# Gates and branch projections with tokens on partitions, and a transposed merge, in a hybrid decoder block

## The chip, the cores and the metric

One core of a Trainium2 chip runs the whole block. The metric is device time in microseconds, the median of several executions; a profile is one further execution recorded by the hardware. TensorE (PE in the profile) multiplies matrices into PSUM, VectorE (DVE) and ScalarE (ACT) do the elementwise work, GpSimd (POOL) nearly nothing here, and SyncE (SP) issues the weight loads. Each engine works through its own instructions in order.

## The reference

One layer over 256 tokens of width 2048, in float32: a mixer sub-layer, then a squared-ReLU MLP. The change lies in the mixer's gates and merge.

```python
h = rms_norm(x, mix_norm_pre) * (1.0 + sc1) + sh1          # sc1, sh1, g1, ... = silu(c) @ w_ada + b_ada
a_q, a_f, a_i, a_g, b_q, b_k, b_v, c_a, c_g = split_cols(h @ w_in, IN_SPLITS)
ya = hgrn2_mixer(...)                # (256, 1024)
yb = dilated_attention_mixer(...)    # (256, 256)
yc = conv_module(...)                # (256, 768)
gates = sigmoid(h @ w_gate + b_gate).reshape(256, 3, 2048)
merged = (gates[:, 0] * (ya @ w_a_out) + gates[:, 1] * (yb @ w_b_out)
          + gates[:, 2] * (yc @ w_c_out))
x = x + g1 * rms_norm(merged @ w_o, mix_norm_post)
h = rms_norm(x, mlp_norm_pre) * (1.0 + sc2) + sh2
x = x + g2 * rms_norm(square(relu(h @ w_up)) @ w_down, mlp_norm_post)
```

## The kernel before

**Jobs.** All weight matrices are cut into chunks of 512 KB (128 partitions x 1024 float32: two k tiles of 128 rows by 512 columns), and each chunk is one job. `run` (L176) goes through one long list of jobs. For each it issues the loads up to five jobs ahead on SyncE's queue into a ring of six raw tiles (`load`, L110), then the splits up to four jobs ahead (`SA`), then the job's own matmuls, then a little side work (`work`, L146). A split (`split`, L117) makes two parts of a weight: ScalarE casts the raw tile to a rounded high part (L126), VectorE subtracts it to give the low part (L127). Activations are kept in the same two parts, and each product takes three matmuls: high x high, high x low, low x high.

**Two forms of a job.** `mm_a` (L240) holds 128 weight columns in the array and moves 256 tokens past them; the result has weight columns on partitions. For a chunk that is 2 k tiles x 4 column tiles x 3 products = 24 matmuls of 256 columns (L252 to L254). `mm_b` (L256) holds 128 tokens and moves 512 weight columns; the result has tokens on partitions: 2 k tiles x 2 token tiles x 3 = 12 matmuls of 512 columns (L264 to L266).

**The order of the jobs.** Input projection with the first adaLN products; then 96 gate jobs (`gj`: four strips n of 512 output columns, in each three branches b of eight chunks; the eight chunks of one (b, n) are a unit), 32 projection jobs (`pj`: in each strip four chunks of ya, one of yb, three of yc), 32 jobs of the output projection (`oj`), 128 of the MLP's up, 128 of its down projection. The list is gates of strips 0 to 2, projection of strip 0, gates of strip 3, projection of strips 1 to 3, output projection. From the 33rd gate job on, 96 adaLN jobs are woven in (L1084): each loads 512 KB too, and VectorE alone multiplies and sums it (L297). When a group of them is done, `g_finish` (L835) writes 2 KB as 4-byte elements to a DRAM scratch (L841) and reads it back as a row on all 128 partitions (L843), both on ScalarE's queue, so that ScalarE stands until the write has landed.

**Side work.** HGRN, attention and convolution are generators in two lists, `chain` (with hand-overs between engines) and `filler` (VectorE alone). After each job `work` takes steps from them, at fixed places of the program:

```python
for _ in range(CH_STEPS):             # CH_STEPS = 2
    c = step(chain)
    if c is None: break
    budget -= c * CH_COST
while budget > 0: ...                 # filler
while budget > 0 and not filler:
    c = step(chain)
    if c is None: break
    budget -= c
```

The instructions are then put in their final order on each engine when the program is built, by a list scheduler that prefers what was written first and can let a later instruction pass one that it expects to wait.

**Gates** (`gate_job`, L814) use `mm_a`. After the eighth chunk ScalarE applies the sigmoid out of PSUM, four times 128x256, with the bias as an operand per partition (L824), which came with the constants. **Projections** (`proj_job`, L859) use `mm_a` too. After a branch's last chunk VectorE multiplies PSUM by the gate (L871) and adds to the strip's sum (L875). After the third branch ScalarE and VectorE split the sum into high and low part (L879, L880); as it has columns on partitions, `o_job` (L947) can hold it in the array directly. The first up unit (`up_job`, L1018) shows a neighbouring form: it is computed with `mm_b`, its relu goes to SBUF, and TensorE transposes it in eight 128x128 pieces (L1048).

**Pools.** `s4`: 28 tiles of 4 KB per partition. `s2`: nine tiles of 2 KB per partition. PSUM: three units of two banks (`ps_unit`) and two single banks (`bank`).

Of the kernel before, what the change touches and what calls it, by code (L numbers as in the profile page):

```python
# [26 lines left out]
# how the work is cut and interleaved  # L27
U0 = 13  # units of the input projection that run along with the first norm's modulation
# [19 lines left out]
for _n, _w in (("c", 16), ("lb", 8), ("b1", 32), ("b2", 32), ("bg1", 16), ("bg2", 16),  # L48
               ("n1", 16), ("n2", 16), ("np1", 16), ("np2", 16), ("bg", 48), ("cw", 186), ("cb", 6), ("lng", 6), ("lnb", 6),
               ("hw", 1)):  # L50
    VEC[_n] = (_o, _o + _w)
    _o += _w
# [4 lines left out]
def hybrid_block(ctx: ExitStack, tc: tile.TileContext, a, out, dbg=None):  # L57
# [57 lines left out]
    gate = []  # instructions that the splits are to come after  # L115
# [14 lines left out]
    chain = []   # (priority, order, generator): work with engine hand-overs, a few steps at a time  # L130
    filler = []  # work of the vector engine alone
# [33 lines left out]
    class Job:  # L165
        def __init__(self, src, shape, fn, ada=False, budget=1.3, keep=0, wait=False, lo_eng=None, extra=False):
            self.src, self.shape, self.fn, self.ada, self.budget = src, shape, fn, ada, budget
            self.keep = keep  # how many jobs later its split weights are let go
            self.wait = wait  # its weights are split by an earlier job's call of ahead(), or when its turn comes
            self.lo_eng = lo_eng  # L170
            self.extra = extra  # its split weights lie in the other pool
            self.raw = self.hl = None
# [54 lines left out]
    def rsqrt_col(dst, parts, scale):  # L227
        """1 / sqrt(scale * sum(parts) + eps), one column: exp(-ln / 2) and a Newton step"""
# [11 lines left out]
    def mm_a(ps, h, l, na, ah, al, first, last, tk=None):  # L240
        """ps[128 cols x 4, 256 tok] += W[kt, cols]^T . act[kt, tok]; na chunks of k in h; tk: one token tile"""
# [14 lines left out]
    def mm_b(ps, h, l, na, ah, al, first, last, tts=(0, 1)):  # L256
        """ps[tt][128 tok, cols] += act[kt, tok]^T . W[kt, cols]"""
# [17 lines left out]
    cbc = []  # silu(c) along the free axis, on every partition  # L275

    def bcast_cols(ps, cols, n):
        """ps[:, j * 128:...] = column j of cols along the free axis, on every partition"""
        for j in range(n):
            nc.tensor.matmul(ps[:, j * P:(j + 1) * P], cols[:, j:j + 1].to_broadcast([P, P]), ident, start=True, stop=True)  # L280
# [8 lines left out]
    def ada_jobs(ct0, n, finish, budget=0.0):  # L289
        """n tiles of 128 output columns on the partitions, two halves of k each along the free axis"""  # L290
# [16 lines left out]
    def ada_pe_jobs(finish):  # L307
        """the first tiles (sc 256 | sh 256) on the tensor engine: 4 groups of k in 4 column groups at once"""
# [24 lines left out]
    def mod_cols(t, kt, dst, b, nw):  # L333
        """dst[:, kt..kt+1, (0, 1)] = (1 + sc) * norm, sh"""
# [9 lines left out]
    xT = []  # L344
    hT = []  # 8 tiles [128, (hi, lo), 2 kt, 256]
# [151 lines left out]
    def lower_bounds():  # L497
        # softmax over the depth axis (one layer), cumulated, less the first layer's
# [34 lines left out]
    vt = [None] * 6  # token-layout units: [b_v 768 | a_i 1024 | a_g 1024]  # L533
# [8 lines left out]
    def hgrn_levels(half):  # L542
        F, Q, K = hg[half]
        A = s4([P, 2, 4, P])  # [s, tile, head, t]
# [97 lines left out]
    def bias_repeat():  # L642
        # row p of head h's square repeats its bias row; read back with a pitch one short, row p is shifted by p
        for h in range(12):
            b0 = bsc[h:h + 1, :]
            nc.scalar.dma_start(brep[h], bass.AP(tensor=b0.tensor, offset=b0.offset, ap=[[0, P], [1, 384]]))

    def bias_rows():
        # B_h[d] = rel_bias[bucket(d), h] where group's pattern allows d, else the mask value
# [113 lines left out]
    # ================= phase 1: first ten input units, streamed with the adaLN strips =================  # L763
# [4 lines left out]
    sj, due = [], {}  # the strips' jobs; how many of them come before the first use of h's pair j  # L768
# [7 lines left out]
    pos = []  # pace of the adaLN jobs: as even as the first uses allow  # L776
# [11 lines left out]
    # ================= phase 2: rest of the input projection (token layout) =================  # L788
# [21 lines left out]
    # ================= phase 3: gates =================  # L810
# [3 lines left out]
    def gate_job(b, n, ch):  # L814
        def fn(h, l):
            if ch == 0:
                pst["gt"] = ps_unit()
            kts = [2 * ch, 2 * ch + 1]
            mm_a(pst["gt"], h, l, 2, [h_hi(k) for k in kts], [h_lo(k) for k in kts], ch == 0, ch == 7)
            if ch == 7:  # L820
                gates[b, n] = s4([P, 4, S])
                for j in range(4):
                    c = b * 16 + n * 4 + j
                    g = nc.scalar.activation(gates[b, n][:, j, :], pst["gt"][:, j // 2, (j % 2) * S:(j % 2 + 1) * S],  # L824
                                             AF.Sigmoid, bias=V("bg")[:, c:c + 1])
                if (b, n) == (2, 3):
                    with tc.issue_after(g.ins):
# [20 lines left out]
    # ================= phase 4: branch projections, gated and merged =================  # L848
    merged = [None] * 4  # F32R [128, (hi, lo) ...]
# [8 lines left out]

    def proj_job(n, ki):  # L859
# [3 lines left out]
        def fn(h, l):  # L863
# [3 lines left out]
            mm_a(pst["pj"], h, l, 2, [t[:, 0, 0, :], t[:, 0, 1, :]], [t[:, 1, 0, :], t[:, 1, 1, :]], first, last)  # L867
            if last:
                g = gates[b, n]
                gv = g.rearrange("p a b -> p (a b)")  # L870
                nc.vector.tensor_mul(gv, pst["pj"].rearrange("p a b -> p (a b)"), gv)  # L871
# [4 lines left out]
                if b == 2:  # L876
                    mh = s4([P, 4, S], F32R)
                    ml = s4([P, 4, S], F32R)
                    nc.scalar.copy(mh, merged[n])  # L879
                    nc.vector.tensor_sub(ml, merged[n], mh.bitcast(F32))  # L880
                    mhl[n] = (mh, ml)
# [5 lines left out]
    # ================= phase 5: output projection, residual, second norm =================  # L887
    x2 = [None] * 4   # [128 tok, tt, 512]
# [18 lines left out]
    h2 = []  # (hi, lo) of four k tiles each  # L907
# [90 lines left out]
    # ================= phase 6: MLP up =================  # L998
# [4 lines left out]
    # order in which the last token tile's chain (p, g), the splits ahead (a) and the first tile's h2 (digits) are traced  # L1003
# [66 lines left out]
    def weave(main, extra):  # L1070
        """main: (jobs, share of the extra ones that goes with each of them)"""
# [19 lines left out]
    # ================= phase 7: MLP down, residual =================  # L1091
# [91 lines left out]
def _chunks(w, kt=2, cols=512):  # L1183
    """[K, N] -> [unit, chunk][128, kt * cols], contiguous"""
# [9 lines left out]
def layout(inputs):  # L1194
# [16 lines left out]
    for k in range(3):  # L1211
# [15 lines left out]
    a["wada0"] = _chunks(cat([sc1[:, :256], sh1[:, :256]], 1))  # L1227
    b = i["b_ada"][0].reshape(6, D)
# [5 lines left out]
        _cols(i["mlp_norm_post"], 16), _cols(i["b_gate"], 48), cw,  # L1234
# [16 lines left out]
```

## Time and profile before

| what | value |
|---|---|
| time, three runs | 1697.65, 1705.83, 1707.48 us |
| median | 1705.83 us |
| span of the profiled execution | 1694.7 us |
| TensorE matmuls | 1636.3 us busy (97%) |
| VectorE | 1163.1 us busy (69%) |
| ScalarE | 745.7 us busy (44%) |
| moved by DMA | 403.31 MB, mean 238 GB/s |

The span goes from the first to the last instruction of one execution. A matmul counts as busy from its start to the modelled end of its result; neighbouring matmuls overlap, so the distance of their starts, not their length, says how fast TensorE goes. Busy shares are means over stages with different limits; the windows and the chain of waits tell what limits one stage. The chain is followed back from the last instruction, at each step to what released it.

### The profile page before, as it was taken

How to read it: one execution, taken by the hardware profiler on the slowest of the kernel's cores; microseconds unless marked ns; L12 is line 12 of the kernel's file. 1: busy time of each engine (PE TensorE's matmuls, PEld its weight loads, DVE VectorE, ACT ScalarE, POOL GpSimd, SP SyncE). 2: the span in 40 equal slices, each digit the busy share in tenths (PEclk: the TensorE clock that was granted, in tenths of full speed). 3: DMA queues.
4: the chain of work that ended last, by engine and by line, in shares of the span. 5: the costliest groups of instructions: out<-in, count | busy, mean ns of one | idle time of the engine just before them, and what ended most of it. 6: DMA issues, size and time to landing. Idle time of an engine off the chain costs nothing.

```text
span 1694.7 us, 27625 instructions
## 1 busy us (share of the span) xinstructions
PE 1636.3 (97%) x11142; PEld 1511.2 (89%) x11142; DVE 1163.1 (69%) x1549; ACT 745.7 (44%) x891; POOL 11.7 (1%) x12
## 2 busy tenths in 40 slices
PE   5999999999999997999999899999999899999997
PEld 4899999878999997999988799999999788888886
DVE  5799979658899885987996755544554655444444
ACT  3644453354454443444444644434343644333333
POOL 0000000000000000000000200000000000000000
PEclk9999999999999999999999999999999999999999
DMA  7999985654344998998898377776767676565662
GB/s 283 323 333 341 326 319 181 205 177 143 101 147 140 290 305 256 360 363 314 284 360 311 125 258 226 231 214 213 247 214 233 208 232 209 190 197 191 194 194 79
DMA packets 120535, 403.31 MB, mean 238 GB/s; under 512 B 17100, under 2 KB 21080, under 8 KB 120408
## 3 DMA queue, kind: packets, MB, share of 16 engines
q1 hardware_dynamic: 107280, 388.24, 68.4%
q10 hardware_dynamic: 13128, 13.31, 2.6%
q8 instruction: 87, 1.43, 0.3%
q14 instruction: 40, 0.33, 0.1%
HBM read 397.28 MB, written 6.59 MB: 238 GB/s over the span
## 4 chain that ended last, share of the span: by engine, by line
PE 79%; DMA 9%; DVE 6%; ACT 3%; issue 2%; ACTq 0%; DVEq 0%; SPq 0%
PE g L254 14%; PE g L252 13%; PE g L253 13%; PE g L1128 5%; PE g L1126 5%; PE g L1127 5%; DMA raw<-wada 5%; PE g L266 4%; PE g L264 4%; PE g L265 4%; DVE lo L127 3%; DMA np_scratch<-adat 2%; PE m L1128 2%; PE m L1126 2%; PE m L1127 2%
## 5 line engine op out<-in xcount | busy, mean ns | idle before, releaser
L126 ACT CAST hi<-raw 128x1024 fp32r<-128x1024 f32 x538 | 561.4, 1051 | 814.9 <-PE g L253 242.6
L127 DVE TENSOR_TENSOR lo<-raw,hi 128x1024 fp32r<-128x1024 f32 x534 | 645.7, 1221 | 316.3 <-ACT hi L126 298.0
L252 PE MATMUL g<-s,hi 128*128 128x256 f32 x2560 | 728.5, 285 | 14.0 <-ACT hi L126 14.0
L254 PE MATMUL g<-s,lo 128*128 128x256 f32 x2560 | 729.2, 285 | 6.3 <-DVE lo L127 6.1
L253 PE MATMUL g<-s,hi 128*128 128x256 f32 x2560 | 727.3, 284 | 0.0
L252 PEld LDWEIGHTS g<-s,hi 128*128 128x128 f32 x2560 | 493.8, 193 | 15.1 <-ACT hi L126 15.0
L254 PEld LDWEIGHTS g<-s,lo 128*128 128x128 f32 x2560 | 493.5, 193 | 9.4 <-DVE lo L127 9.3
L253 PEld LDWEIGHTS g<-s,hi 128*128 128x128 f32 x2560 | 493.6, 193 | 0.0
L297 DVE SCALAR_TENSOR_TENSOR raw<-raw,s 128x1024 f32<-128x1024 f32 x184 | 224.0, 1219 | 130.8 <-DMA raw<-wada 130.6
L1126 PE MATMUL g<-hi,s 128*128 128x512 f32 x384 | 149.4, 389 | 0.0
L1127 PE MATMUL g<-lo,s 128*128 128x512 f32 x384 | 149.4, 389 | 0.0
L1128 PE MATMUL g<-hi,s 128*128 128x512 f32 x384 | 149.4, 389 | 0.0
L266 PE MATMUL g<-hi,s 128*128 128x512 f32 (+1 forms) x344 | 132.9, 386 | 2.9 <-DVE s L940 2.9
L264 PE MATMUL g<-hi,s 128*128 128x512 f32 (+1 forms) x344 | 132.3, 385 | 0.0
L265 PE MATMUL g<-lo,s 128*128 128x512 f32 (+1 forms) x344 | 131.6, 382 | 0.3 <-DVE lo L127 0.3
L1128 PEld LDWEIGHTS g<-hi,s 128*128 128x128 f32 x384 | 72.1, 188 | 15.0
L1127 PEld LDWEIGHTS g<-lo,s 128*128 128x128 f32 x384 | 72.0, 188 | 15.0
L1126 PEld LDWEIGHTS g<-hi,s 128*128 128x128 f32 x384 | 72.1, 188 | 14.8
L266 PEld LDWEIGHTS g<-hi,s 128*128 128x128 f32 x344 | 65.0, 189 | 18.2 <-DVE s L940 3.8
L450 DVE SCALAR_TENSOR_TENSOR s<-s,vec,s 128x256 f32<-128x256 f32 x180 | 77.6, 476 | 0.0
L264 PEld LDWEIGHTS g<-hi,s 128*128 128x128 f32 x344 | 65.1, 189 | 13.7 <-issue 1.6
L265 PEld LDWEIGHTS g<-lo,s 128*128 128x128 f32 x344 | 65.1, 189 | 12.8 <-DVE lo L127 0.8
(204 smaller groups left out, 1024.7 us busy)
## 6 DMA issues: line engine op xcount, KB each, us to landing
raw<-wada SPq DMA_DIRECT2D x192, 512.0 KB, 5.5
raw<-wu SPq DMA_DIRECT2D x128, 512.0 KB, 4.7
raw<-wd SPq DMA_DIRECT2D x128, 512.0 KB, 4.3
raw<-wg SPq DMA_DIRECT2D x96, 512.0 KB, 5.0
raw<-w SPq DMA_DIRECT2D x80, 512.0 KB, 5.0
raw<-wv SPq DMA_DIRECT2D x44, 512.0 KB, 4.5
raw<-wp SPq DMA_DIRECT2D x32, 512.0 KB, 5.1
raw<-wo SPq DMA_DIRECT2D x32, 512.0 KB, 5.3
```

The costliest lines, as they stand in the source:

```text
L126: nc.scalar.copy(h, raw)
L127: (eng or nc.vector).tensor_sub(l, raw, h.bitcast(F32))
L252: nc.tensor.matmul(o, h[:, i, w], x, start=f and b0, stop=False, skip_group_check=True)
L253: nc.tensor.matmul(o, h[:, i, w], y, start=False, stop=False, skip_group_check=True)
L254: nc.tensor.matmul(o, l[:, i, w], x, start=False, stop=e and b1, skip_group_check=True)
L264: nc.tensor.matmul(o, ah[i][:, tk], h[:, i, :], start=f, stop=False)
L265: nc.tensor.matmul(o, ah[i][:, tk], l[:, i, :], start=False, stop=False)
L266: nc.tensor.matmul(o, al[i][:, tk], h[:, i, :], start=False, stop=e)
L297: nc.vector.scalar_tensor_tensor(raw, raw, 1.0, cbc[q % 2], op0=ALU.mult, op1=ALU.mult, accum_out=st["p"][:, q:q + 1])
L1126: nc.tensor.matmul(o, uh[:, kt % 4, tk], h[:, 0, w], start=kt == 0, stop=False)
L1127: nc.tensor.matmul(o, uh[:, kt % 4, tk], l[:, 0, w], start=False, stop=False)
L1128: nc.tensor.matmul(o, ul[:, kt % 4, tk], h[:, 0, w], start=False, stop=kt == 63)
```

## The change

Both `gate_job` and `proj_job` call `mm_b` in place of `mm_a`. The gate's bias now varies along the free axis: it is loaded for each unit as one row of 512 values repeated on all partitions (256 KB, into an `s2` tile, on ScalarE's queue, at the unit's first chunk), VectorE adds it out of PSUM, and ScalarE takes one sigmoid of 128x1024 in SBUF. The 48 bias columns leave the constants. The merged sum has tokens on partitions, so a new generator `merge_gen`, at the head of the side list, waits four steps and then, for two halves, transposes four 128x128 pieces on TensorE into a PSUM bank, copies the high part on ScalarE and subtracts for the low part on VectorE. Beside this, only comments were taken out.

```diff
     def gate_job(b, n, ch):
         def fn(h, l):
             if ch == 0:
                 pst["gt"] = ps_unit()
+                pst["gb"] = s2([P, 512])
+                b0 = a["bgate"][0:1, b * D + n * 512:b * D + (n + 1) * 512]
+                nc.scalar.dma_start(pst["gb"], bass.AP(tensor=b0.tensor, offset=b0.offset, ap=[[0, P], [1, 512]]))
             kts = [2 * ch, 2 * ch + 1]
-            mm_a(pst["gt"], h, l, 2, [h_hi(k) for k in kts], [h_lo(k) for k in kts], ch == 0, ch == 7)
+            mm_b(pst["gt"], h, l, 2, [h_hi(k) for k in kts], [h_lo(k) for k in kts], ch == 0, ch == 7)
             if ch == 7:
-                gates[b, n] = s4([P, 4, S])
-                for j in range(4):
-                    c = b * 16 + n * 4 + j
-                    g = nc.scalar.activation(gates[b, n][:, j, :], pst["gt"][:, j // 2, (j % 2) * S:(j % 2 + 1) * S],
-                                             AF.Sigmoid, bias=V("bg")[:, c:c + 1])
+                g = gates[b, n] = s4([P, 2, 512])
+                nc.vector.tensor_add(g, pst["gt"], pst["gb"][:, None, :].to_broadcast([P, 2, 512]))
+                e = nc.scalar.activation(g, g, AF.Sigmoid)
...
+    def merge_gen(n):
+        for _ in range(MERGE_WAIT):
+            yield 0.0
+        mh, ml = s4([P, 4, S], F32R), s4([P, 4, S], F32R)
+        mhl[n] = (mh, ml)
+        for q in range(2):
+            ps = bank()
+            for j in range(2):
+                for t in range(2):
+                    nc.tensor.transpose(ps[:, j * S + t * P:j * S + (t + 1) * P],
+                                        merged[n][:, t, (2 * q + j) * P:(2 * q + j + 1) * P], ident)
+            psv = ps.rearrange("p (a b) -> p a b", a=2)
+            k = slice(2 * q, 2 * q + 2)
+            nc.scalar.copy(mh[:, k, :], psv)
+            nc.vector.tensor_sub(ml[:, k, :], psv, mh[:, k, :].bitcast(F32))
+            yield 0.6
+
+    MERGE_WAIT = 4
...
     def proj_job(n, ki):
...
-            mm_a(pst["pj"], h, l, 2, [t[:, 0, 0, :], t[:, 0, 1, :]], [t[:, 1, 0, :], t[:, 1, 1, :]], first, last)
+            mm_b(pst["pj"], h, l, 2, [t[:, 0, 0, :], t[:, 0, 1, :]], [t[:, 1, 0, :], t[:, 1, 1, :]], first, last)
             if last:
                 g = gates[b, n]
-                gv = g.rearrange("p a b -> p (a b)")
-                nc.vector.tensor_mul(gv, pst["pj"].rearrange("p a b -> p (a b)"), gv)
+                nc.vector.tensor_mul(g, pst["pj"], g)
...
                 if b == 2:
-                    mh = s4([P, 4, S], F32R)
-                    ml = s4([P, 4, S], F32R)
-                    nc.scalar.copy(mh, merged[n])
-                    nc.vector.tensor_sub(ml, merged[n], mh.bitcast(F32))
-                    mhl[n] = (mh, ml)
+                    add_side(-1, merge_gen(n))
```

## Rows read from the trace of the kernel before

**Rows 1.** The page's head: span of the profiled execution.

```profile
span 1694.7 us, 27625 instructions
```

**Rows 2.** Windows: us, busy (xinstructions) per engine, clock, DMA share, GB/s.

```profile
390.00:566.00 176.00, 172.77 (x1395) 167.02 (x1394) 158.91 (x290) 76.31 (x128) 0.00 (x0) 1.00 0.47 155
566.00:695.00 129.00, 118.93 (x931) 116.88 (x930) 96.81 (x147) 54.55 (x76) 0.00 (x0) 0.96 0.94 292
715.00:784.00 69.00, 69.00 (x577) 69.00 (x576) 59.20 (x82) 29.19 (x33) 0.00 (x0) 1.00 0.98 362
784.00:853.00 69.00, 69.00 (x577) 69.00 (x576) 59.60 (x71) 30.07 (x31) 0.00 (x0) 1.00 0.82 275
```

**Rows 3.** Chain of waits by line: 390:566, 566:695, 680:830 us.

```profile
by line: PE m L564 14.2%; PE g L252 12.4%; PE g L253 12.3%; PE g L254 12.1%; DVE lo L127 5.4%; issue 4.5%; DVE s L450 3.7%; PE g L266 3.0%; DMA s<-bias_rows 2.9%; PE g L264 2.7%; DMA raw<-wg 2.7%; PE g L265 2.7%; PE m L548 2.3%; PE m L712 2
...
by line: DMA np_scratch<-adat 20.5%; DMA raw<-wada 17.0%; PE g L254 12.3%; PE g L253 12.0%; PE g L252 11.9%; DVE lo L127 4.7%; issue 4.5%; DMA raw<-wg 4.3%; DVE raw L297 4.2%; ACT hi L126 2.5%; PE m L469 2.2%; PE m L459 2.0%; ACTq L843 0.5%
...
by line: PE g L252 33.4%; PE g L253 33.4%; PE g L254 33.3%
```

**Rows 4.** Waits, 566 to 695 us: engine, line, releaser: us, times, longest.

```profile
ACT hi L126 <- DMA np_scratch<-adat: 22.7, 2, 12.9
```

**Rows 5.** Timeline of TensorE, projection and gates, 256 columns: start, us, line, shape.

```profile
713.33 0.28 PE L252 MATMUL g<-s,hi 128*128 128x256 f32 x1
...
716.93 0.28 PE L252 MATMUL g<-s,hi 128*128 128x256 f32 x1
```

**Rows 6.** Timeline of TensorE in the down projection, 512 columns.

```profile
1400.07 0.39 PE L1126 MATMUL g<-hi,s 128*128 128x512 f32 x1
...
1405.96 0.39 PE L1128 MATMUL g<-hi,s 128*128 128x512 f32 x1
```

**Rows 7.** Groups by line and form: count | busy us, mean ns | idle before.

```profile
L824 ACT ACTIVATE s<-g,vec 128x256 f32<-128x256 f32 x48 | 18.7, 475 | 3.1 <-PE g L254 3.1
...
L1059 ACT ACTIVATE s<-s 128x1024 f32<-128x1024 f32 x15 | 15.9, 1059 | 0.4
```

**Rows 8.** Timeline of VectorE, strips 0, 2 and 3 of the projection.

```profile
717.29 1.22 DVE L871 TENSOR_TENSOR s<-g,s 128x1024 f32<-128x1024 f32 x1
718.43 1.21 DVE L127 TENSOR_TENSOR lo<-raw,hi 128x1024 fp32r<-128x1024 f32 x1
719.56 1.22 DVE L875 TENSOR_TENSOR s<-s,s 128x1024 f32<-128x1024 f32 x1
...
818.65 1.23 DVE L871 TENSOR_TENSOR s<-g,s 128x1024 f32<-128x1024 f32 x1 [0.61 <-PE g L254]
...
832.95 1.22 DVE L875 TENSOR_TENSOR s<-s,s 128x1024 f32<-128x1024 f32 x1
...
857.57 1.21 DVE L875 TENSOR_TENSOR s<-s,s 128x1024 f32<-128x1024 f32 x1
```

**Rows 9.** Instructions on the scratch tile: ns min/median/max, first and last start.

```profile
L843 ACTq DMA_DIRECT2D s<-np_scratch x8: 326/329/339, 595.2 to 1318.9; - x8
```

**Rows 10.** Windows: ten microseconds of the output projection.

```profile
870.00:880.00 10.00, 10.00 (x45) 8.26 (x45) 9.51 (x17) 5.07 (x8) 0.00 (x0) 1.00 1.01 408
```

**Rows 11.** Timeline of TensorE at the first up unit's eight transposes.

```profile
977.83 0.28 PE L252 MATMUL g<-s,hi 128*128 128x256 f32 x1
...
978.91 0.28 PE L252 MATMUL g<-s,hi 128*128 128x256 f32 x1
979.11 1.09 PE L1048 MATMUL m<-ident,s 128*128 128x128 f32 x8
979.96 0.36 PE L253 MATMUL g<-s,hi 128*128 128x256 f32 x1
```

**Rows 12.** Timeline: a gate unit's sigmoids; strip 3's last matmul.

```profile
761.05 1.57 ACT L824 ACTIVATE s<-g,vec 128x256 f32<-128x256 f32 x4 [1.14 <-PE g L254]
...
852.89 0.28 PE L254 MATMUL g<-s,lo 128*128 128x256 f32 x1
```

More of the change, by code (lines that the diff above doesn't have):

```diff
@@ L48 @@
 for _n, _w in (("c", 16), ("lb", 8), ("b1", 32), ("b2", 32), ("bg1", 16), ("bg2", 16),
-               ("n1", 16), ("n2", 16), ("np1", 16), ("np2", 16), ("bg", 48), ("cw", 186), ("cb", 6), ("lng", 6), ("lnb", 6),
+               ("n1", 16), ("n2", 16), ("np1", 16), ("np2", 16), ("cw", 186), ("cb", 6), ("lng", 6), ("lnb", 6),
                ("hw", 1)):
@@ L817, in fn @@
                 pst["gt"] = ps_unit()
+                pst["gb"] = s2([P, 512])
+                b0 = a["bgate"][0:1, b * D + n * 512:b * D + (n + 1) * 512]
+                nc.scalar.dma_start(pst["gb"], bass.AP(tensor=b0.tensor, offset=b0.offset, ap=[[0, P], [1, 512]]))
             kts = [2 * ch, 2 * ch + 1]
-            mm_a(pst["gt"], h, l, 2, [h_hi(k) for k in kts], [h_lo(k) for k in kts], ch == 0, ch == 7)
+            mm_b(pst["gt"], h, l, 2, [h_hi(k) for k in kts], [h_lo(k) for k in kts], ch == 0, ch == 7)
             if ch == 7:
-                gates[b, n] = s4([P, 4, S])
-                for j in range(4):
-                    c = b * 16 + n * 4 + j
-                    g = nc.scalar.activation(gates[b, n][:, j, :], pst["gt"][:, j // 2, (j % 2) * S:(j % 2 + 1) * S],
-                                             AF.Sigmoid, bias=V("bg")[:, c:c + 1])
+                g = gates[b, n] = s4([P, 2, 512])
+                nc.vector.tensor_add(g, pst["gt"], pst["gb"][:, None, :].to_broadcast([P, 2, 512]))
+                e = nc.scalar.activation(g, g, AF.Sigmoid)
                 if (b, n) == (2, 3):
-                    with tc.issue_after(g.ins):
+                    with tc.issue_after(e.ins):
                         st_ln.append(nc.scalar.preload_act_table_set("natural_log_exp_and_others"))
@@ L1227, in layout @@
     a["wada0"] = _chunks(cat([sc1[:, :256], sh1[:, :256]], 1))
+    a["bgate"] = np.ascontiguousarray(i["b_gate"])
     b = i["b_ada"][0].reshape(6, D)
@@ L1233, in layout @@
         _cols(b[5], 16), _cols(i["mix_norm_pre"], 16), _cols(i["mlp_norm_pre"], 16), _cols(i["mix_norm_post"], 16),
-        _cols(i["mlp_norm_post"], 16), _cols(i["b_gate"], 48), cw,
+        _cols(i["mlp_norm_post"], 16), cw,
         _cols(i["conv_b"], 6), _cols(i["conv_ln_g"], 6), _cols(i["conv_ln_b"], 6), _cols(i["hgrn_norm_w"], 1)], 1))
```

## The prediction

> **What bounds the kernel now.** I read the head of the page first for the profiled execution's span, 1694.7 us [rows 1]; the three timed runs were 1697.65, 1705.83 and 1707.48, so it lies 3.0 under the fastest and 11.1 under the median. The change touches 96 gate jobs and 32 projection jobs, so I next cut the trace into four stretches by windows [rows 2]: A, 390 to 566 us, the first 32 gate jobs beside HGRN, attention and convolution work; B, 566 to 695, the next 40 with about one adaLN load per job woven in; C, 715 to 784, the last 24, woven the same way; D, the projection: 24 jobs in 784 to 853, eight just ahead of C. The reader sees TensorE busy without a break in C and D, 10 us idle in B and 3 in A; VectorE at 90% in A; the DMA share at 94% and 98% in B and C, 47% in A.
>
> Busy is not bound, so the chain of waits is cut the same way [rows 3]. In A some 37% of the chain is gate matmuls, the rest mostly side work of TensorE and VectorE. In B 36% is gate matmuls; more is transfers and a small scatter to DRAM which ScalarE waits out: 22.7 us in two waits [rows 4]. In C and D it is nothing but the moved matmuls.
>
> **The matmuls.** Before, a job has 24 matmuls (2 k tiles x 4 column tiles x 3 products) of 256 columns. They start 0.120 us apart (31 starts, 30 steps: 3.60/30) [rows 5]: 24 x 0.120 = 2.88 us. After, it has 12 (2 x 2 token tiles x 3) of 512 columns, the form that the down projection runs; there starts lie 0.2265 apart (27 starts, 26 steps: 5.89/26) [rows 6]: 2.72 us. So a job saves 0.162 us (5.6%), and 128 jobs 20.7. The halved weight loads add nothing: they lie under matmuls, and the starts count them already.
>
> The Trainium skill ("TensorE: Matmul & The Clock Gate", Back-to-back issue gap) gives N/2.4 + 2.5 ns for a warm matmul: 109 and 216 ns, so 0.03 us a job and only 4 us in all. The trace says 120 and 226.5, and the measurement decides; the rule speaks against the change and is the last rival.
>
> **What each stretch keeps of it.**
> A: 32 x 0.162 = 5.2 at most. Gate matmuls are 36.8% of 176 us = 64.8 us of the chain, of the jobs' 92; I take that part, 64.8 x 5.6% = 3.6. Against it stands VectorE: a unit's bias, until now an operand of four sigmoids on ScalarE (0.475 us each [rows 7]), becomes a 128x1024 addition out of PSUM on VectorE. The nearest row is the gate product, also 128x1024 from PSUM: starts 1.14 apart [rows 8]. Four units: 4.6 us. VectorE's lines carry some 15% of A's chain by my estimate from the two listed (5.4 and 3.7%) and the small ones: 0.7. A: -2.9; ends -5.2 and -3.6 + 4.6 = +1.0.
>
> ScalarE instead does one sigmoid of 128x1024 per unit, about 1.06 by the nearest row [rows 7], in place of 1.9. I cost this gain at nothing: ScalarE is busy 43% of A [rows 2]. The sigmoid now waits for the addition; behind it stand later splits, but four split jobs lie ahead for TensorE, 4 x 2.72 = 10.9 us, against 1.14 + 1.06. The addition waits on VectorE for the unit's last matmul where ScalarE waited before, with the same cover; once it is gone, each microsecond of wait would be one of TensorE.
>
> B: the matmuls' part of the chain is 36.2% of 129 us = 46.7; 5.6% of it is 2.6. Against it: each unit loads its bias row onto 128 partitions, 256 KB, issued on ScalarE's queue, like the broadcast of G1 (0.33 us per issue [rows 9], hidden in ScalarE's idle time; nothing waits for the data for some seven jobs). Five units are 1.3 MB, at this stretch's 292 GB/s 4.5 us; since 6% of the DMA time (7.7 us) is free there, I take 1.5. And the lead in front of ScalarE's two long waits shrinks by 4 x 0.162 = 0.65 us each: 1.3. B: +0.2; ends -2.6 and +5.8 (no gain, both losses whole).
>
> C: 24 x 0.162 = 3.9. A job with its share of adaLN loads (0.955) and bias moves 1.955 x 0.524 + 0.033 = 1.058 MB, in 2.72 us 389 GB/s; C ran at 362 [rows 2], while ten microseconds of the output projection held 408 [rows 10]. VectorE would have 59.2 + 3 x 1.14 = 62.6 us of 65. I take 70%: -2.7; ends -3.9 and, at 362 (2.92 us a job), +1.0.
>
> D: 32 x 0.162: -5.2. The DMA share of 82% leaves room. VectorE's split of the merged result becomes two halves out of PSUM, about the same work; ScalarE's copy likewise.
>
> **The transposes.** Merged now has tokens on partitions and must be turned: 8 per strip n, 32 in all. The one place with the same eight is the first up unit [rows 11]: its eight start at 979.11, the next matmul at 979.96, and the matmul ahead of them began at 978.91 and needs until 979.03: 0.93 us. Two groups with a switch each: 1.0, four times: +4.0.
>
> What are they late for? They need the product and the sum of the strip's last branch. By the text they wait four steps of the side queue; but `work` runs right behind the job, takes two steps of cost 0, then, the filler being empty by then, goes on stepping while budget is left: all four waits and both groups are traced at once. So the wait does nothing. In rows 11 the transposes were traced at once as well, yet next-unit matmuls stand between (first at 977.83, last at 978.91): the built order leaves room for the producer. How much room here, no row shows. VectorE ran product, a split, sum [rows 8]; room for these three is 3 x 1.14 = 3.4 us. The real lag, from TensorE's last result to the end of the sum: strip 0: ScalarE got a gate unit 16 jobs later at 761.05 [rows 12], so the end was 761.05 - 46.1 = 715.0, the sum ended at 720.8: 5.8. Strip 2: the first product came at 818.65 straight on its matmul, four jobs ahead of the end, 830.2; sum until 834.2: 4.0; strip 1 shows the same. Strip 3: last matmul at 852.89 + 0.28, sum until 858.8: 5.6. Together 19.4; less 4 x 3.4 it is 5.7 us of TensorE standing still: my term, nearest to that order; ends 0 and 19.4.
>
> **Sum:** -2.9 + 0.2 - 2.7 - 5.2 + 4.0 + 5.7 = -0.9 us: span 1693.8; on the median, 1704.9, so 1705.
>
> **Rivals.**
> (1) The gain arrives: A and C whole, no standing still: -5.2 - 2.6 - 3.9 - 5.2 + 4.0 = -12.9, 1693. For it: C and D are all matmuls; against it: lags of 4 to 5.8 us.
> (2) The other side: the transposes stand right behind the strip's last matmul and hold TensorE for the whole lag: -0.9 - 5.7 + 19.4 = +12.8, 1719. It decides once the room left is under about 3.2 us per strip: 4 x 0.2 eats the 0.9. For it: the empty wait; against it: rows 11.
> (3) Transfers cap B and C: B +5.8, C +1.0: sum +8.4, 1714. It decides if sustained DMA stays under some 377 GB/s (2.805 us a job, a gain of 1.8 in C). For it: 98% in C; against it: 408 held. The Trainium skill ("DMA: Bandwidth & Descriptors", Where 436 GB/s comes from) says HBM binds at about 358 GB/s; by that C would not gain. Rows 10 speak against it.
> (4) VectorE becomes the bound through the additions: A +1.0, C and D no gain: +10.9, 1717. It is full in no stretch [rows 2], so little speaks for it.
> (5) The new jobs start their matmuls at twice 0.120: no saving anywhere (14.1 lost): +13.2, 1719. Rows 6 speak against it.
>
> **How the numbers follow.** Forecast (-6 to +7) 50%, rival 1 18%, rival 2 15%, 3 and 4 7% each, 5 3%. Its own range is 1699 to 1713. With some 3 us of scatter between executions, the range that leaves out about two in ten is 1692 to 1722: rival 1 is mostly in, rivals 2 and 5 just. A change of 1% (17 us) is about what a measurement of this kernel tells from none. Faster by that needs more than rival 1 and some of B: 6%. Slower needs rival 2 with 3 (+22) or a worse order: 12%. Within 1%: 82%.
>
> **What would show it.** In the profile after: matmuls of 512 columns 0.2265 apart in C and D; the 3072 gate and projection matmuls halved to 1536, and 32 more transposes; TensorE's idle time ahead of the transposes, released by the sum on VectorE, near 1.4 us a strip (0: rival 1; over 4: rival 2); C shortened from 69 to about 66, with ScalarE's waits for the gates' loads grown if rival 3 holds; VectorE idle in A down by some 4 us. The forecast is wrong if the built order puts the side work elsewhere: A's HGRN chain has steps on three engines and I moved none of them.

## The result, and the profile after

Median of 17 runs each on the same chip: after 1709.53 us (1704.53 to 1712.97), before 1700.42 (1692.78 to 1708.14); after to before 1.0051, 95% interval 1.0035 to 1.0067. The kernel became some 9 us slower: a small loss, but one that the interval tells from no change, where 0.9 us of gain was forecast. The time lies inside the stated range and within 1%; as a change, +9 us lies outside the -6 to +7 that the forecast took for its own, and it goes the other way. The profiled executions stand 9.6 apart: 1694.7 [rows 1] and

```profile
span 1704.3 us, 24604 instructions
```

I cut the trace of after as before was cut. B ends later now, so it is shown in three parts, and C and D are moved.

Windows of after: start:end and length, us; busy us (x instructions) of TensorE, its weight loads, VectorE, ScalarE, GpSimd; granted clock, DMA share, GB/s. A, three parts of B, C, D, and the output projection.

```profile
390.00:566.00 176.00, 173.49 (x995) 148.48 (x993) 159.53 (x288) 74.36 (x119) 0.00 (x0) 1.00 0.48 148
566.00:620.00 54.00, 46.55 (x178) 35.69 (x177) 46.69 (x76) 24.53 (x32) 0.00 (x0) 0.91 0.91 276
620.00:660.00 40.00, 25.64 (x99) 19.98 (x97) 17.78 (x26) 8.71 (x9) 0.00 (x0) 0.83 1.04 229
660.00:712.00 52.00, 41.64 (x159) 32.15 (x160) 32.95 (x45) 15.14 (x15) 0.00 (x0) 0.86 0.93 285
733.50:800.60 67.10, 66.45 (x297) 54.86 (x296) 58.71 (x82) 27.06 (x27) 0.00 (x0) 1.00 0.95 359
800.60:868.50 67.90, 67.25 (x305) 55.53 (x305) 65.36 (x75) 32.48 (x33) 0.00 (x0) 1.00 0.87 302
868.50:930.00 61.50, 61.44 (x276) 50.75 (x275) 54.29 (x76) 27.39 (x34) 0.00 (x0) 1.00 0.99 372
```

Set against [rows 2]: A is as before, C and D are full of TensorE work with fewer instructions (297 in 67.10 us for 577 in 69.00). B is where it went: TensorE is busy 25.64 of the 40 us in the middle, the DMA engines show full (1.04), and yet only 229 GB/s arrive. The granted clock there is 0.83.

The chain of waits of after, 566 to 695 us, by line (against the second line of [rows 3]):

```profile
by line: DMA np_scratch<-adat 27.7%; DMA raw<-wg 14.9%; DVE lo L127 10.0%; PE g L265 8.8%; PE g L266 7.9%; PE g L264 7.1%; DVE raw L297 6.9%; issue 5.9%; DMA s<-np_scratch 4.8%; ACT hi L126 4.1%; ACTq L821 1.6%; DVE s L484 1.5%; DVE s L476 
```

The three gate matmul lines hold 23.8% of the chain instead of 36.2%; the write of G1's pieces to DRAM scratch (`np_scratch<-adat`) 27.7% instead of 20.5%, the read back (`s<-np_scratch`) 4.8%, which was not in the chain before. The gates' own weight loads (`raw<-wg`) hold 14.9% instead of 4.3%, but the adaLN loads (17.0% before) are no longer in it: weight loads together went from 21.3% to 14.9%. Now the waits that carry it.

Waits of after, 558 to 712 us: engine, line, releaser; us in all, times, longest (against [rows 4]).

```profile
ACT hi L126 <- DMA raw<-wg: 55.3, 23, 7.4
...
ACT hi L126 <- issue: 33.9, 3, 12.5
...
PE g L264 <- ACT hi L126: 26.7, 7, 9.5
...
PE g L265 <- DVE lo L127: 5.9, 9, 1.3
```

and of before, the same window:

```profile
ACT hi L126 <- DMA raw<-wg: 36.5, 19, 3.9
```

The line `<- issue` is ScalarE held by the scratch read at the head of its queue: three such stands, 33.9 us (before 26.8, also three: the 22.7 of [rows 4] and 4.1 at line L486; the longest 12.9 before, 12.5 after). ScalarE waits 55.3 us for gate loads where it waited 36.5. New is what TensorE waits: 26.7 us for ScalarE's halves of the splits and 5.9 for VectorE's. Before, from 566 to 720 us, TensorE waited 10.1 us; after, 32.2.

One stand shows how. Timeline of ScalarE in after: start and duration, us; line; idle time before it in brackets.

```profile
643.35 1.06 ACT L827 ACTIVATE s<-s 128x1024 f32<-128x1024 f32 x1 [1.83 <-DVE s L826]
644.55 0.39 ACTq L843 DMA_DIRECT2D np_scratch<-adat  x1
645.06 1.05 ACT L126 CAST hi<-raw 128x1024 fp32r<-128x1024 f32 x1 [0.65 <-PE g L266]
657.70 0.35 ACTq L845 DMA_DIRECT2D s<-np_scratch  x1
658.08 0.45 ACTq L821 DMA_DIRECT2D s<-bgate  x1
658.65 2.94 ACT L126 CAST hi<-raw 128x1024 fp32r<-128x1024 f32 x3 [12.53 <-issue]
664.68 1.05 ACT L126 CAST hi<-raw 128x1024 fp32r<-128x1024 f32 x1 [3.09 <-DMA raw<-wg]
```

The scratch write is issued at 644.55, one more split is done (645.06 + 1.05 = 646.11), and then the queue stands until 657.70, when the data have landed and the read can go. The unit's new bias load (L821) goes behind it, then three splits at once. TensorE in the same stretch:

```profile
649.85 0.39 PE L266 MATMUL g<-hi,s 128*128 128x512 f32 x1
659.75 0.79 PE L264 MATMUL g<-hi,s 128*128 128x512 f32 x1 [9.50 <-ACT hi L126]
...
662.03 0.63 PE L264 MATMUL g<-hi,s 128*128 128x512 f32 x1
662.45 0.63 PE L265 MATMUL g<-lo,s 128*128 128x512 f32 x1
662.88 0.63 PE L266 MATMUL g<-hi,s 128*128 128x512 f32 x1
...
663.73 0.46 PE L265 MATMUL g<-lo,s 128*128 128x512 f32 x1
664.03 0.39 PE L266 MATMUL g<-hi,s 128*128 128x512 f32 x1
```

TensorE had matmuls until 659.75 - 9.50 = 650.25: 4.1 us after the last split. Then it stood 9.50 us. At the same stand of the kernel before, the last split ended at 631.16 and TensorE had matmuls until 645.15 - 4.02 = 641.13, a lead of 10.0; it stood 4.02 us of a stand of the same length. ScalarE in the kernel before:

```profile
629.10 0.38 ACTq L841 DMA_DIRECT2D np_scratch<-adat  x1
630.10 1.06 ACT L126 CAST hi<-raw 128x1024 fp32r<-128x1024 f32 x1 [1.51 <-DMA raw<-wg]
643.61 0.33 ACTq L843 DMA_DIRECT2D s<-np_scratch  x1
644.06 1.99 ACT L126 CAST hi<-raw 128x1024 fp32r<-128x1024 f32 x2 [12.90 <-DMA np_scratch<-adat]
```

and TensorE:

```profile
640.85 0.28 PE L254 MATMUL g<-s,lo 128*128 128x256 f32 x1
645.15 0.38 PE L252 MATMUL g<-s,hi 128*128 128x256 f32 x1 [4.02 <-ACT hi L126]
```

So this stand is not new, nor longer. What is gone is the lead with which TensorE came into it. The other two stands of after were followed by waits of TensorE of 4.4 and 7.4 us, those of before by 0.6 and 3.4.

The milestones (strip ends by VectorE's first work on the strip's last unit) give the balance. The end of B's last gate unit: before 715.0 - 8 x 2.88 = 692.0 (the eight projection jobs of strip 0 lie behind it, [rows 12]); after, by VectorE's row

```profile
711.72 1.23 DVE L826 TENSOR_TENSOR s<-g,s 128x1024 f32<-128x1024 f32 x1 [0.31 <-PE g L266]
```

711.7: 19.7 later. In A, counted by gate matmuls, after had got 1.25 jobs further by 566 us (37.0 jobs to 35.75), 3.5 us ahead. Of these, 1.6 were there when the gates began (first gate matmul at 420.33 before, 418.73 after). So: up to the end of A -3.5, **B +23.2**, strip 0's projection -1.2 (23.0 to 21.8), C -1.9 (69.0 to 67.1), D -1.3 (69.2 to 67.9), all that comes later -5.7; together +9.6.

### The profile page after: what moved, and what is told of

Read it like the earlier page. It is cut to its first block, busy times and chain, and to the rows that moved or that the text cites. A ratio compares the mean times of both kernels' runs of the same rounds, so it can differ in the third digit from the quotient of the medians.

```text
span 1704.3 us, 24604 instructions
## 1 busy us (share of the span) xinstructions
PE 1631.5 (96%) x9638; PEld 1436.7 (84%) x9638; DVE 1176.0 (69%) x1565; ACT 739.5 (43%) x859; POOL 12.5 (1%) x12
## 4 chain that ended last, share of the span: by engine, by line
PE 77%; DMA 10%; DVE 8%; ACT 3%; issue 2%; ACTq 0%; DVEq 0%; SPq 0%
PE g L254 9%; PE g L252 9%; PE g L253 9%; PE g L265 8%; PE g L266 8%; PE g L264 7%; PE g L1144 5%; PE g L1145 5%; PE g L1143 5%; DMA np_scratch<-adat 3%; DVE lo L127 3%; DMA raw<-wg 2%; PE m L1145 2%; PE m L1143 2%; PE m L1144 2%
## 5 line engine op out<-in xcount | busy, mean ns | idle before, releaser
L254 PE MATMUL g<-s,lo 128*128 128x256 f32 x1536 | 437.6, 285 | 2.9 <-DVE lo L127 2.9
L252 PE MATMUL g<-s,hi 128*128 128x256 f32 x1536 | 436.7, 284 | 1.7 <-ACT hi L126 1.7
L253 PE MATMUL g<-s,hi 128*128 128x256 f32 x1536 | 436.6, 284 | 0.0
L264 PE MATMUL g<-hi,s 128*128 128x512 f32 (+1 forms) x856 | 337.8, 395 | 26.7 <-ACT hi L126 26.7
L265 PE MATMUL g<-lo,s 128*128 128x512 f32 (+1 forms) x856 | 338.0, 395 | 7.6 <-DVE lo L127 7.6
L266 PE MATMUL g<-hi,s 128*128 128x512 f32 (+1 forms) x856 | 337.5, 394 | 2.1 <-DVE s L957 2.1
L254 PEld LDWEIGHTS g<-s,lo 128*128 128x128 f32 x1536 | 296.6, 193 | 4.7 <-DVE lo L127 4.6
L252 PEld LDWEIGHTS g<-s,hi 128*128 128x128 f32 x1536 | 296.6, 193 | 2.0 <-ACT hi L126 1.9
L253 PEld LDWEIGHTS g<-s,hi 128*128 128x128 f32 x1536 | 296.6, 193 | 0.0
L264 PEld LDWEIGHTS g<-hi,s 128*128 128x128 f32 x856 | 163.9, 191 | 63.2 <-ACT hi L126 29.5
L265 PEld LDWEIGHTS g<-lo,s 128*128 128x128 f32 x856 | 163.6, 191 | 45.0 <-DVE lo L127 13.1
L266 PEld LDWEIGHTS g<-hi,s 128*128 128x128 f32 x856 | 163.6, 191 | 36.9 <-DVE s L957 3.0
L1143 PEld LDWEIGHTS g<-hi,s 128*128 128x128 f32 x384 | 72.1, 188 | 14.9
L1144 PEld LDWEIGHTS g<-lo,s 128*128 128x128 f32 x384 | 72.1, 188 | 14.9
L1145 PEld LDWEIGHTS g<-hi,s 128*128 128x128 f32 x384 | 72.2, 188 | 14.8
```

The costliest lines, as they stand in the source:

```text
L252: nc.tensor.matmul(o, h[:, i, w], x, start=f and b0, stop=False, skip_group_check=True)
L253: nc.tensor.matmul(o, h[:, i, w], y, start=False, stop=False, skip_group_check=True)
L254: nc.tensor.matmul(o, l[:, i, w], x, start=False, stop=e and b1, skip_group_check=True)
L264: nc.tensor.matmul(o, ah[i][:, tk], h[:, i, :], start=f, stop=False)
L265: nc.tensor.matmul(o, ah[i][:, tk], l[:, i, :], start=False, stop=False)
L266: nc.tensor.matmul(o, al[i][:, tk], h[:, i, :], start=False, stop=e)
```

## The experiments

Before, the projected pieces of G1 are spread over the partitions through DRAM: a write of 512 elements of 4 bytes, a wait, a read. The change leaves that alone; but it stands in B. I held four explanations against each other: the time goes with ScalarE's stand at the scratch read; the new bias loads and additions take it directly; loads are what limits B, because the scratch writes hold them up, so that each new transfer and lost lead counts; the additions stall the queues by their wait. The runs came in three sets of four (e1 to e4, e5 to e8, e9 to e12), each beside runs of the kernel before on the same chip; ratios are to those, with their 95% intervals.

**Move the stand away.** Both kernels with the scratch read issued 16 jobs later, when the write has long landed:

```diff
-            G[i] = s2([P, 512])
-            nc.scalar.dma_start(G[i], bass.AP(...))
+            def read():
+                G[i] = s2([P, 512])
+                with tc.issue_after(last_cast[0].ins):
+                    nc.scalar.dma_start(G[i], bass.AP(...))
+            pend.append([16, read])   # counted down after each job
```

> The changed kernel, with the read back of the adaLN scratch row (G1, G2) issued 16 jobs after its write instead of right behind it, so that ScalarE no longer stands until the write has landed. Theory S (the change lost its gain because ScalarE's stand in the scratch reads now meets TensorE with little split work ahead: three waits of 10 to 12.5 us, TensorE idle 22.5 us in the three gaps behind them): 20 to 25 us faster than the changed kernel, TensorE's idle time from 566 to 712 us falls from 32 to about 10. Theory B (the bias rows' extra 3.1 MB is what B cannot carry): the transfers stay, so at most 8 to 12 us faster.

> The kernel before with the same late read. Theory S: it had two such waits of 12.9 and 9.8 us but more lead, TensorE idle 4.3 and 3.7 us behind them, and 5.0 once in the up projection: 8 to 14 us faster than before, and slower than the changed kernel with the late read by 4 to 10 us. Theory B: as fast or faster than the changed kernel with the late read, since it moves 3.1 MB less.

Measured: after 0.9965 (0.9946 to 0.9985; 1688.17 us), before 0.9873 (0.9848 to 0.9897; 1675.19), both beside 1694.98. Without the stand both are faster, before by 21 us, after by 1.0051 - 0.9965, 15 us. But the changed kernel stays 13 us behind the unchanged one: more than the 9 it lost with the stand in place. (If the stand were all, it would now be the faster one.) The stand costs time in both; it does not make the difference between them. The explanation by the stand alone falls. Neither gain is the size that was expected: after's 15 lies between the figures of theories S and B, and before's 21 above the 8 to 14 of S. That the kernel before is the faster one with the late read is what theory B had said. TensorE's waits from 566 to 720 us fell to 17.7 and 3.7.

**Take parts of the bias path away.** One bias row loaded once and used for all units (e3); no load and no addition (e4):

```diff
-                pst["gb"] = s2([P, 512])
-                nc.scalar.dma_start(pst["gb"], ...)        # each unit
+                if not gb0:                                 # e3: one load in all
+                    gb0.append(s2([P, 512])); nc.scalar.dma_start(gb0[0], ...)
+                pst["gb"] = gb0[0]
...
-                nc.vector.tensor_add(g, pst["gt"], ...)
-                e = nc.scalar.activation(g, g, AF.Sigmoid)
+                e = nc.scalar.activation(g, pst["gt"], AF.Sigmoid)   # e4, and no load
```

> The changed kernel with one bias row loaded once, ahead of the gates, and used for all twelve units (the other eleven rows are left out, so the gates take a wrong bias). The additions stay, 2.9 MB of loads go, also the ones that stand straight behind the scratch reads. Theory S: the stands of 10 to 12 us stay, 2 to 6 us faster than the changed kernel. Theory B: 15 us or more faster.

> The changed kernel without a bias at all: no load, no addition on VectorE, ScalarE takes the sigmoid straight out of PSUM (the bias is left out of the result). Against the run with one bias row it gives what the twelve additions cost. Theory S: within 3 us of that run, 3 to 8 us faster than the changed kernel. A theory that VectorE's additions hold up the splits: 12 us or more faster than the run with one row.

Measured: e3 1.0001 (0.9979 to 1.0023), e4 0.9954 (0.9927 to 0.9980). From 1.0051, the eleven loads are worth 0.0050 of 1700, 8.5 us, the twelve additions another 0.0047, 8 us; and the matmuls and transposes alone bring 7.8 us of gain (each known to about 5 us only, by the intervals). So the wide matmuls do pay, and the bias path costs some twice what they bring: 16.5 us for 3 MB of loads and 12 x 1.22 us of additions. That is most of what these would cost if nothing covered them: at the 292 GB/s of [rows 2], eleven loads are 9.9 us of transfer, and twelve additions are 14.6 us of VectorE, although only five of the twelve units lie in B. Both are more than theory S had expected (2 to 6 for the loads, at most 3 for the additions). Why so little of it is covered was the next question.

**Take the scratch away.** G1 and G2 spread by four TensorE products with the identity instead, one copy out of PSUM, no write, no read:

```diff
-            d = gsc[nw]
-            nc.scalar.dma_start(d[4 * i:4 * i + 4, :].rearrange("j p -> p j"), t)
-            G[i] = s2([P, 512])
-            nc.scalar.dma_start(G[i], bass.AP(...))
+            ps = bank()
+            bcast_cols(ps, t, 4)
+            G[i] = s2([P, 512])
+            nc.scalar.copy(G[i], ps)
```

> The kernel before with the adaLN gate rows (G1, G2) spread over the partitions by four small TensorE products with the identity, in place of the 4-byte write to DRAM and the read back: no scratch transfer at all. Theory L (B is bound by loads; each 4-byte write holds every load for about 10 us, in which 130 to 260 GB/s arrive instead of 360 to 400): 20 to 26 us faster than before (the late read alone gave 20), wg and wada landing times no longer reach 10 us. Theory S (only ScalarE's stand counts): the same as the late read, 18 to 21 us faster than before.

> The changed kernel with the same spreading on TensorE. Theory L: TensorE's waits in 560 to 700 us fall from 17 (late read) to under 8, 10 to 16 us faster than the changed kernel with the late read, level with the kernel before with the same spreading within 6 us. Theory S: as the late read, within 4 us of it.

Measured: before 0.9900 (0.9866 to 0.9934; 1673.21 to 1677.13 us), after 0.9867 (0.9834 to 0.9900; 1667.52 to 1671.40). The order turns: without the scratch the changed kernel is the faster of the two, 5.5 us by the ratios or the medians (1676.00 and 1670.56, on one chip; the ranges of the runs don't touch, the intervals of the ratios do). TensorE's waits from 566 to 720 us are 0 and 6.0 us. This is what the loads' explanation asks: take out the small writes, and B carries the change. One thing speaks for less: before gained 17 us, below what either theory had named, and no more than e2 with the writes still in (0.9873). In the kernel before, once the stand is away, taking out the writes gains nothing that can be told (e5's own products and copies are in that); in after it gains 17 us beside the stand's 15 (0.9965 to 0.9867).

**Double the writes.** The kernel of e2 (before, read moved away) with each write issued a second time to another scratch; nobody reads the copy, and no wait is added:

```diff
             nc.scalar.dma_start(d[4 * i:4 * i + 4, :].rearrange("j p -> p j"), t)
+            nc.scalar.dma_start(gsc2[nw][4 * i:4 * i + 4, :].rearrange("j p -> p j"), t)
```

> The kernel before with the late read, and each 2 KB write of 4-byte elements issued twice, the second time to a scratch that nobody reads (no engine waits for it). Theory L: each write holds the loads for some 10 us at about half rate, four more of them in B: TensorE's waits in 566 to 720 us grow from 3.7 to 15 or 25, 10 to 20 us slower than the late read with one write. Theory S (only ScalarE's stand counts): within 3 us of it.

Measured: 1.0148 (1.0115 to 1.0180; 1716.51 us) where e2 had 0.9873: eight more writes of 2 KB cost 2.75%, some 46 us (39 by the profiled spans, 1673.0 and 1712.0). The window from 566 to 660 us, columns as above, of e5 (no writes):

```profile
566.00:660.00 94.00, 94.00 (x769) 93.30 (x768) 85.05 (x130) 49.32 (x70) 0.00 (x0) 1.00 0.94 335
```

of e2 (writes, read moved away) and of after:

```profile
566.00:660.00 94.00, 91.75 (x730) 90.59 (x729) 76.24 (x120) 42.57 (x60) 0.00 (x0) 0.98 0.95 297
566.00:660.00 94.00, 72.19 (x275) 55.66 (x273) 64.47 (x101) 33.24 (x41) 0.00 (x0) 0.88 0.96 256
```

of e9 (twice as many writes):

```profile
566.00:660.00 94.00, 84.03 (x649) 82.48 (x648) 65.83 (x104) 38.92 (x57) 0.00 (x0) 0.96 0.98 242
```

and of before and of e6, the changed kernel without writes:

```profile
566.00:660.00 94.00, 87.82 (x695) 86.26 (x694) 72.46 (x113) 41.89 (x61) 0.00 (x0) 0.98 0.92 281
```

```profile
566.00:660.00 94.00, 88.97 (x397) 71.20 (x396) 84.92 (x130) 44.72 (x54) 0.00 (x0) 1.00 0.93 334
```

The share of busy DMA time hardly moves (0.92 to 0.98), the rate goes from 335 GB/s without writes over 297 (281 in before) with them to 242 with twice as many, and TensorE's busy time with it: 94.00, 91.75 (87.82), 84.03. The changed kernel gets from 256 GB/s to 334, and from 72.19 us busy to 88.97. The share is no measure of room. A lower rate alone could also mean that fewer loads were asked for. The loads' own times speak against that. Of the gates' and adaLN loads issued from 566 to 700 us, all of 512 KB, those from 3 us before to 9 us after the issue of such a write took 10.2 us to land in the median in before, 10.8 in after and 12.0 in e9; the others took 5.4, 5.7 and 6.9, and all of them 5.1 in e5 and 5.6 in e6 (those whose landing the trace has; in e9 only five and four). DMA queues from 617 to 626 us, where after has a write out: queue, packets, MB, share of the 16 engines; q1 has the weight loads, q10 the write.

```profile
q1 hardware_dynamic: 448, 1.62, 118.8%
q10 hardware_dynamic: 528, 0.00, 3.3%
```

and the weight loads of e5, the same window:

```profile
q1 hardware_dynamic: 936, 3.41, 98.6%
```

So the write's own pieces take 3.3%. The share is full because each packet of the loads beside them is under way more than twice as long. Twice ten microseconds of after in which such a write is out most of the time:

```profile
620.00:630.00 10.00, 5.79 (x26) 4.47 (x24) 2.91 (x5) 0.92 (x1) 0.00 (x0) 0.99 1.01 113
650.00:660.00 10.00, 0.50 (x3) 0.25 (x1) 0.27 (x1) 1.35 (x2) 0.00 (x0) 0.68 0.90 84
```

and ten of e9:

```profile
610.00:620.00 10.00, 7.13 (x60) 6.93 (x58) 8.32 (x13) 8.05 (x16) 0.00 (x0) 1.00 1.15 121
```

113 and 84 GB/s, and 121, at shares around one. In e9, B's end (the first load for the projection) came 16.7 us later than in e2 (690.5 to 673.8). TensorE's waits from 566 to 720 us grew from 3.7 to 16.2 us, as expected; the whole loss is more than the 10 to 20 us expected. The rest of it lies later, where the other four writes are doubled too: VectorE's waits for adaLN loads from 900 us on grew from 136.1 us (longest 9.4) to 153.8 (longest 17.9), and TensorE stood 17.5 us in two waits for a split.

**Move the addition and the sigmoid three jobs later,** so that nothing in the queues waits for a unit's last matmul; beside the scratch (e7) and without it (e8):

```diff
-                nc.vector.tensor_add(g, pst["gt"], ...)
-                e = nc.scalar.activation(g, g, AF.Sigmoid)
+                def evac():
+                    nc.vector.tensor_add(g, gt, ...); e = nc.scalar.activation(g, g, AF.Sigmoid)
+                pend.append([3, evac])
```

> The changed kernel, scratch as it was, with each gate unit's addition and sigmoid written three jobs later (PSUM holds the unit longer). Theory V (the addition on VectorE and then the sigmoid on ScalarE wait for TensorE's last matmul with loaded weights queued behind them, so the ring of raw tiles stands; leaving bias and addition out gave 9 us more than one bias row did): 5 to 10 us faster than the changed kernel. If the addition costs by VectorE's time alone: within 2 us of the changed kernel.

> The changed kernel with the spreading on TensorE and the later addition and sigmoid. Theories L and V together: 25 to 35 us faster than the changed kernel, level with or up to 8 us below the kernel before with the spreading, since only the bias loads and the 32 transposes stand against the matmuls' gain of 20.7. If the change has a cost that none of these touches: over 5 us slower than the kernel before with the spreading.

Measured: e7 1.0068 (1.0043 to 1.0094), e8 0.9892 (0.9860 to 0.9925): no gain over 1.0051 and 0.9867. Waits of e7, 558 to 712 us:

```profile
ACT hi L127 <- DMA raw<-wg: 69.4, 27, 9.4
...
PE g L270 <- ACT hi L127: 22.9, 4, 7.2
ACT hi L127 <- issue: 11.3, 1, 11.3
...
ACT hi L127 <- DMA np_scratch<-adat: 9.4, 1, 9.4
```

ScalarE's stands at the scratch read, which have two names here, went down to 20.7 us (33.9 in after) while its waits for loads went up to 69.4 (55.3 in after), and TensorE still waits 22.9 us for its splits (26.7 in after). The explanation by the additions' wait falls.

**The bias path without the scratch.** e6 with one bias row loaded once (e10), with neither load nor addition (e11), and with the rows spread by TensorE from the 48 bias columns, which go back among the constants, so that the whole computation stands with no bias load (e12):

```diff
-                nc.scalar.dma_start(pst["gb"], ...)                     # e12
+                bcast_cols(pst["gp"], V("bg")[:, c:c + 4], 4)
+                nc.scalar.copy(pst["gb"], pst["gp"])
```

> The changed kernel with the spreading on TensorE and one bias row for all units (the other eleven rows are left out, so the gates take a wrong bias). With the scratch gone B has transfers to spare, so the bias loads should be nearly hidden: 2 to 6 us faster than with twelve loads (TensorE's waits in B 6.0 there). If the bias loads cost as much as beside the scratch writes (7 us): 6 to 9 us faster.

> The changed kernel with the spreading on TensorE, no bias loads and no additions (the bias is left out of the result): what the moved matmuls and the transposes alone bring. The saving of 20.7 us less 3.5 for the transposes, of which A gave some 5, C and D some 9: 8 to 14 us faster than the kernel before with the spreading, 2 to 8 us faster than with one bias row. If the additions cost as much as beside the scratch writes: 9 us faster than with one bias row.

> The changed kernel with both the adaLN rows and the gate biases spread by TensorE: four small products per unit into a PSUM bank, a copy on ScalarE (0.6 us), no bias load; the addition stays. TensorE gains 12 x 0.6 = 7 us of work, the DMA loses 3.1 MB: within 5 us of the changed kernel with the spreading and the bias loads, 12 to 20 us faster than before.

Measured: 0.9874 (0.9845 to 0.9902), 0.9850 (0.9818 to 0.9882), 0.9899 (0.9864 to 0.9933), to e6's 0.9867. Without the scratch the loads cost nothing that can be told (2 to 6 us were expected), and the additions at most a few microseconds (e10 to e11: 4, intervals overlap). The matmuls and transposes alone, e11 to e5, bring 0.0050, 8.5 us, give or take 8: not to be told from the 7.8 beside the scratch. e12 saves nothing more. So nothing says that the gain differs between the settings; the price of the bias path does: 16.5 us (give or take 5) beside the scratch writes and about 3 (give or take 8) without them (e6 to e11).

The two best that compute the whole are e6 (0.9867) and e2 (0.9873), both under either kernel of the change.

## Why the prediction failed, point by point

**B is the step that failed.** It was put at +0.2 (ends -2.6 and +5.8) and is +23.2. Three of its steps were wrong. First, "since 6% of the DMA time (7.7 us) is free there, I take 1.5": the share said nothing of room. At nearly the same share the rate is 335 GB/s without the writes and 281 with them, so B was limited by its loads wherever a write was out, and 1.3 MB more had no free time to go into. That the lead "shrinks by 4 x 0.162 = 0.65 us each": the lead was put at the jobs' saving; at the stand shown it went from 10.0 to 4.1 us. The likely reason is that with loads as the limit faster matmuls only use the lead up sooner, while the splits wait for data (55.3 us of waits for gate loads, 36.5 before). These waits alone are not the loss: e6, with more of them (62.6 from 566 to 720 us), lets TensorE wait 6.0 us. And the additions were priced in A alone; in B their cover ("four split jobs lie ahead") was a lead that was mostly gone, and they cost 8 us in all. What I had in hand and didn't put together: [rows 2] has B at a share of 0.94 with 292 GB/s, while C has 0.98 with 362. Nearly the same share, 70 GB/s apart, and 20.5% of B's chain under a write of 2 KB [rows 3]. That was a sign that the writes slow the loads beside them.

Of B's 23.2 us, the waits of TensorE are 22.1 (32.2 - 10.1). Behind long waits TensorE also starts slowly: behind the 9.50 us shown, starts lie 0.425 us apart until 663.73 (662.03 to 663.73, 4 steps) and 0.2285 later (664.95 to 667.92, 13 steps), some 1.6 us for eight starts. In the timeline from 566 to 720 us, 51 starts lie 0.41 to 0.60 us apart, nearly all in five runs behind waits, and cost 11.0 us over 0.2266 each; before, 41 starts of 256 columns cost 4.5 us over 0.120 each. That is 6.5 us more, as much as the 40 jobs save; 1.1 us stays open.

The Trainium skill ("DMA: Bandwidth & Descriptors", Specifications) asks for at least 512 bytes per transfer for line rate, below which the engine does read-modify-write. The runs show a transfer of such pieces as slow: 2 KB took 10.4 to 13.1 us to land in after. The read-modify-write itself no run here shows. What such a write takes from the loads beside it the page doesn't price; e9 does, at 46 us for eight.

**Rival 3** (transfers cap B and C, +8.4) named the right cause in B and the wrong size, 5.8 for 23.2; and C was not capped: it ran at 359 GB/s with TensorE full. The Trainium skill ("DMA: Bandwidth & Descriptors", Where 436 GB/s comes from) puts the limit at about 358; the output projection of after held 372 over 61.5 us (last window above), so the trace doesn't bear that out as a cap.

**That the whole came out near the forecast is luck.** B alone is 23.0 us worse than forecast; 12.7 of that came back in strip 0's projection and D (7.0 better than forecast) and in what no step foresaw (5.7).

**A** was put at -2.9; -3.5 measured by its end, -1.9 from the first gate matmul on. But VectorE's idle time there did not fall by 4 us (busy 158.91 before, 159.53 after, in a window that holds 1.25 jobs more); that forecast row failed, and how the additions are covered in A was not looked into.

**C** was put at -2.7; -1.9 measured. The matmuls of 512 columns start 0.2266 apart there (7.25 us for 32 steps), as the down projection's do (0.2265). Timeline of TensorE in after:

```profile
744.62 0.39 PE L265 MATMUL g<-lo,s 128*128 128x512 f32 x1
...
751.87 0.39 PE L264 MATMUL g<-hi,s 128*128 128x512 f32 x1
```

Rival 5 is out: starts lie neither at twice 0.120 nor at the 0.216 that was weighed with the matmuls.

**D and the transposes.** Forecast -5.2 for the matmuls, +4.0 and +5.7 for the transposes. Strip 0's projection and D came out 2.5 us shorter. The transposes are the other misjudged term, on the good side. Strip 2's, timeline of TensorE in after:

```profile
828.13 0.39 PE L265 MATMUL g<-lo,s 128*128 128x512 f32 x1
828.36 1.03 PE L871 MATMUL m<-ident,s 128*128 128x128 f32 x8
829.15 0.48 PE L266 MATMUL g<-hi,s 128*128 128x512 f32 x1
```

Eight take 829.15 - 828.36 = 0.79 us, and the row ahead of them has no idle time: the built order had put matmuls of the next jobs between the sum and the transposes. In the whole kernel TensorE stood before them once:

```profile
  DVE s L896: 0.5, 1
```

0.5 us in place of 5.7; in all 4 x 0.8 + 0.5 = 3.7 us in place of 9.7, if the other three strips' eight take as long. Rival 2 (the whole lag, 19.4) is out. Room was there, as [rows 11] hinted; I had taken the smaller room that I could count.

**The rest** came out 5.7 us shorter, which no step foresaw. TensorE's waits from 920 to 1660 us fall from 14.5 to 8.0, mostly those for ScalarE's halves (5.9 in two to 1.7 in one). This is one execution of each; what caused it stays open.

**Rival 1** (the gain arrives) did not come in the kernel as it is. Without the scratch the changed kernel is 5.5 us faster; its matmuls and transposes alone bring some 8 us in both pairs of runs, of the 12.9 that the rival named.

What stays open: why the additions alone cost 8 us beside the scratch writes. That they add to a chain that has no lead is the likely reading; e7 showed only that their wait in the queue is not it.

## What to carry to other kernels

Read the DMA share beside the GB/s and the loads' times to landing: B, at a share of 0.94 with 20% less rate than its neighbour, was limited by transfers, whatever the idle share said, and there a faster TensorE gained little and loads and operations that seemed covered were paid for. Price a small-element write by what the loads beside it lose (compare the rate with and without it), not by its bytes. Turning tokens onto partitions turns a bias per partition, which is an operand of the sigmoid, into a load and an addition per unit: price both in every stretch in which units end.

## What the runs showed of the hardware

A write of 512 elements of 4 bytes, 2 KB, was under way for 10.9 us in the median (10.4 to 13.1 in the four of after's eight whose landing the trace has). Ten microseconds with such a write out for most of them moved 84 to 121 GB/s, at a DMA share of 0.90 to 1.15, and loads of 512 KB beside it took 10 to 12 us to land where they took 5 to 7 otherwise; with no such write the kernels moved 334 and 335 GB/s from 566 to 660 us. Eight more of them cost 46 us (39 by the profiled spans). After a wait of 9.50 us TensorE's 512-column matmuls started 0.425 us apart (its level of 1.2 GHz) for about eight, then 0.2285 (2.4 GHz); the granted clock of 566 to 712 us is 0.96 before and 0.87 after.
